# The residual summed into PSUM behind the first expert product, and normalised rows stored with even and odd columns apart

## The chip, the core and the metric

The kernel runs on one core of one Trainium2 chip. The core has a matrix engine (PE, TensorE), which loads a stationary operand (LDWEIGHTS) and streams a moving one through it (MATMUL) into PSUM; a vector engine (DVE), a scalar engine (ACT) and GpSimd (POOL), which read and write SBUF; and DMA queues, here fed almost wholly by SyncE (SP). The metric is the time of the whole program on the device in microseconds: 1033.31, the median of three runs of the kernel before (1030.22 to 1036.1).

## What is computed

Two decoder layers over 256 rows of 1024 columns, all in float32. Each layer is a set of four attention mixers, then a mixture of 32 experts of which each row uses two. The change lies in the experts. Cut to what matters:

```python
def hier_moe(h, w_coarse, b_coarse, w_fine, b_fine, w13, w2):
    lc = xf @ w_coarse + b_coarse
    grp = argmax(lc)                       # one of 4 groups
    lf = (xf @ w_fine + b_fine)[its group] # 8 experts in it
    top_p, top_e = top_k(softmax(lf), 2)
    wts = p_grp * top_p / sum(top_p)
    # per expert e: rows that chose it
    a, b = split(x_rows @ w13[e]);  y = (silu(a) * b) @ w2[e]
    # summed back into the rows with wts
x <- x + gate2(c) * hier_moe(rms_norm(x) * (1 + scale2(c)) + shift2(c))
```

## The kernel before, in words

The weights of the 32 experts of a layer are some 100 MB (32 experts of 2 MB in `w13` and 1 MB in `w2`), and all are read in each layer. They come in pieces of 1 MB into one of 8 ring buffers, or of 0.5 MB into one of 29 SBUF "pages" (128 by 1024 float32). SP issues these loads strictly in the order of a list (`advance`, line 302); a load waits until its buffer is free, which is when the last product that read the buffer's former piece is through (`done`, line 327). At most eight such loads are in flight.

All instructions are issued in the order in which the Python code calls them; each engine runs its own in that order, and semaphores order them between engines. The stretch that the change touches is `experts` (line 2071):

1. `router_part(l, 3)` transposes the last columns of the residual `X` on PE, ACT scales them into SBUF, and its second half `mm()` multiplies them with the router's weights.
2. `seeds(t)` opens the four PSUM banks `acc` in which the experts' results are summed: it multiplies the residual `X[t]` with the identity, two matmuls of 512 columns in float32 for each `t`, and so puts `x` itself into the sum. `seeds(0)` stands between the transposes and `mm()`, `seeds(1)` behind `route`.
3. `rstd_of` (DVE) gives `rs`, one factor a row. ACT writes `hh`, the rounded product `X * rs`, in four instructions of 512 columns; DVE writes `hl`, what the rounding left over, in eight of 256 columns (`lo(q)`: both `t` of one quarter `q`).
4. `route` (line 1852) is a chain of small DVE instructions from the router's sums to `rk`, the place of each row in its expert's list. `lo(0)` is called inside it, while PE adds up counts (`tri`). After it come `prep_sel(0)`, which builds 0/1 matrices `sel` from `rk`, and `lo(1)` to `lo(3)`, all on DVE.
5. `gather_bank` (line 1968) gathers the rows of the experts by matmul: for each block `kt` of 128 columns the stationary operand is a block of `hh` or `hl`, the moving one is `sel`. The block's columns are every second column of a range of 256 (`by_twos`, line 544), since the weights' rows are stored in pairs. Each bank of two blocks takes eight matmuls of 256 columns in the order hh, hl of `t=0`, hh, hl of `t=1`; four banks make a gather.
6. Eight steps `p` follow, each for four experts: `first(p, 0)`, `first(p, 1)` (products with `w13`), the gate on ACT and DVE, `second` (products with `w2`), and `scatter`, which adds into `acc`. Step 0 has `prep_t(0)` behind its first product (transposes of `sel`, slot weights). Gathers for later experts lie between the products.

Before the experts the mixers run an order of steps written out by hand; the change does not touch it.

Of the kernel before, what the change touches and what calls it, by code (L numbers as in the profile page):

```python
# [14 lines left out]
AF = mybir.ActivationFunctionType  # L15
OP = mybir.AluOpType
# [242 lines left out]
def kernel(ctx, tc, x_in, c_in, w_ada, b_ada, norm_gain, w_in, qk_gain, cmp_pe, cmp_w1, cmp_w2,  # L259
# [4 lines left out]
    V, A, G, T = (Engine(M, e, g) for e, g in zip("VAGP", (nc.vector, nc.scalar, nc.gpsimd, nc.tensor)))  # L264
# [7 lines left out]
    def dap(t, off, ap):  # L272
        return bass.AP(tensor=t.tensor, offset=t.offset + off, ap=ap)
# [3 lines left out]
    def T_(tag, shape, dt=FT):  # L277
        t = sb.tile(shape, dt, name=tag, tag=tag, bufs=TAGS[tag])
        M.tile(tag, TAGS[tag], t.tensor.name)
        return t  # L280

    def pg(shape, dt=FT):
        return T_("pg", shape, dt)

    def at(shape, dt=FT):
        t = ps.tile(shape, dt, name="at", tag="at", bufs=4)
        M.tile("at", 4, t.tensor.name)
        return t

    def mmb():  # L290
        t = ps.tile([128, 512], FT, name="mm", tag="mm", bufs=4)
        M.tile("mm", 4, t.tensor.name)
        return t
# [88 lines left out]
    X = {}  # L382
# [161 lines left out]
    def by_twos(v, kt):  # L544
        return v[:, 256 * (kt // 2) + kt % 2:256 * (kt // 2) + 256:2]
# [116 lines left out]
    def rstd_of(ss, eng=None):  # L662
        s2 = sm(2)
        V.tensor_reduce(s2, ss.rearrange("p (s t) -> p t s", t=2), axis=AX.X, op=OP.add)
        return rsqrt(s2, 2, 1.0 / D, eng or V)
# [39 lines left out]
    H = {}  # L705
# [757 lines left out]
    def expert(p, b, s):  # L1463

        return p + 16 * b + 8 * s
# [502 lines left out]
    def gather_bank(l, sel, n, q, xg, eng):  # L1968
        m = 64 * n
        p = at([128, 2, m])  # L1970
        for i in range(2):
            kt = 2 * q + i
            c = 0
            for t in range(2):
                for src in (H["hh"], H["hl"]):
                    T.matmul(p[:, i], by_twos(src[t], kt), sel[:, t].rearrange("p e s -> p (e s)"),
                             start=c == 0, stop=c == 3)
                    c += 1
        for i in range(2):
            kt = 2 * q + i  # L1980
            a, b = MOD[l, "A2"][:, kt:kt + 1], MOD[l, "sh2"][:, kt:kt + 1]
            if eng is V:
                V.tensor_scalar(xg[kt // 4][:, kt % 4], p[:, i], a, b, op0=OP.mult, op1=OP.add)
            else:
                A.activation(xg[kt // 4][:, kt % 4], p[:, i], AF.Identity, bias=b, scale=a)

    def first_half(p, m):
        t = T_("gt", [128, 512])
        A.activation(t, p, AF.Copy, scale=m)
        return t  # L1990
# [80 lines left out]
    def experts(l):  # L2071
        units = ada_pe(l, 5)

        def filler(n):
            for _ in range(n):
                units.pop(0)[1]()


        acc = {}

        def seeds(t):
            acc[t] = [mmb(), mmb()]
            for n in range(2):
                T.matmul(acc[t][n], ID, X[t][:, 512 * n:512 * n + 512], start=True, stop=False)

        filler(1)
        mm = router_part(l, 3)
        seeds(0)
        rs = rstd_of(H["ss"])
        for i in ("hh", "hl"):  # L2090
            H[i] = [pg([128, D], FR) for _ in range(2)]

        def lo(q):
            for t in range(2):
                c = slice(256 * q, 256 * q + 256)
                V.scalar_tensor_tensor(H["hl"][t][:, c], X[t][:, c], rs[:, t:t + 1], H["hh"][t][:, c], op0=OP.mult,
                                       op1=OP.subtract)

        for h in range(2):
            for t in range(2):  # L2100
                c = slice(512 * h, 512 * h + 512)
                A.activation(H["hh"][t][:, c], X[t][:, c], AF.Copy, scale=rs[:, t:t + 1])
        mm()
        filler(4)
        most, further, weights = route(l, rs, lo)
        seeds(1)

        NP = NE // 4
        SEL, ST, SW, SM, XG = {}, {}, {}, {}, {}

        def prep_sel(q):
            SEL[q], ST[q] = selection(rk[:, :, 4 * q:4 * q + 4], 4)
            XG[q] = [pg([128, 4, 256]) for _ in range(2)]

        def prep_t(q):
            selection_t(SEL[q], ST[q], 4)
            SW[q], SM[q] = slot_weights(SEL[q], W[:, :, :, 4 * q:4 * q + 4], 4)

        def prep_g(q, b, eng=None):
            gather_bank(l, SEL[q], 4, b, XG[q], eng or (V if b % 2 else A))  # L2120

        def first(p, b):
            q, i = divmod(p, 2)
            h = at([128, 512])
            for k in range(KT):
                for e in range(2):
                    key = "w13", l, expert(p, b, e), k // 4
                    c = 128 * i + 64 * e
                    T.matmul(h[64 * e:64 * e + 64], XG[q][k // 4][:, k % 4, c:c + 64], piece(key, (k % 4) * 512, 512),
                             start=k == 0, stop=k == KT - 1)  # L2130
                if k % 4 == 3:
                    for e in range(2):
                        done(("w13", l, expert(p, b, e), k // 4))
            return h

        def masks(p):
            return [SM[p // 2][:, b, p % 2:p % 2 + 1] for b in range(2)]

        def second(p, gT):
            ys = [at([128, 512]) for _ in range(2)]  # L2140
            for b in range(2):
                for n in range(2):
                    for k in range(2):
                        for e in range(2):
                            w = tiles[("w2", l, expert(p, b, e), k)]
                            T.matmul(ys[n][64 * e:64 * e + 64], gT[:, b, k, 64 * e:64 * e + 64],
                                     w[:, 512 * n:512 * n + 512], start=b == 0 and k == 0, stop=b == 1 and k == 1)
                    if b:
                        ys[n] = weighted(ys[n], SW[p // 2][:, p % 2:p % 2 + 1], MOD[l, "g2"][:, 512 * n:512 * n + 512])
                for k in range(2):  # L2150
                    for e in range(2):
                        done(("w2", l, expert(p, b, e), k))
            return ys

        prep_sel(0)
        most()
        for i in range(1, 4):
            lo(i)
        free["pg"] += P4[l]
        advance()  # L2160
        for b in range(4):
            prep_g(0, b, V if b > 1 else A)
        further()
        weights()
        ys = None
        for p in range(NP):
            q, i = divmod(p, 2)
            nxt = q + 1 < NP // 2
            if nxt and i == 0:
                prep_sel(q + 1)  # L2170
            if l + 1 < DEPTH and p == 2:
                load_weights(l + 1)
                load_cw2(l + 1)
            if l + 1 < DEPTH and p == NP - 1:
                tables()
            h = first(p, 0)
            if p == 0:
                prep_t(0)
            h = first_half(h, masks(p)[0])
            g = swiglu(first(p, 1), h, masks(p))  # L2180
            if p == 0:
                filler(2)
            if p:
                scatter(acc, ST[(p - 1) // 2][:, (p - 1) % 2], ys, False)
            if nxt:
                prep_g(q + 1, 3 * i)
            gT = hidden_t(g)
            if nxt and i == 0:
                prep_g(q + 1, 1)
                prep_g(q + 1, 2)  # L2190
            elif nxt:
                prep_t(q + 1)
            ys = second(p, gT)
        more_rounds(l, acc)
        scatter(acc, ST[q][:, i], ys, True)
        last = l == DEPTH - 1
        for t in range(2):
            X[t] = pg([128, D])
        for n in range(2):
            for t in range(2):  # L2200
                c = slice(512 * n, 512 * n + 512)
                if t:
                    A.activation(X[t][:, c], acc[t][n], AF.Copy)
                else:
                    V.tensor_copy(X[t][:, c], acc[t][n])
            for t in range(2):
                c = slice(512 * n, 512 * n + 512)
                if last:
                    nc.sync.dma_start(dap(out, t * 128 * D + 512 * n, [[D, 128], [1, 512]]), X[t][:, c])
            if not last:  # L2210
                turn(n)
# [56 lines left out]
```

## Time and profile before

| What | us |
|---|---|
| median of three runs | 1033.31 |
| the profiled execution's own time | 1038.59 |
| its span, first to last instruction | 1037.0 |
| PE busy | 982.9 |
| DVE busy | 538.9 |
| ACT busy | 406.5 |
| stretch of the experts in layer 0 / layer 1, from the first gather to the end of the results, about | 305 to 528 / 808 to 1037 |

The profile is of one execution. Almost all instructions carry the line of one helper (L253), so instructions are told apart by operation, shape and tile: `mm<-pg,K` are the seeds (identity `K`, residual in a page), `at<-pg` of 128x256 the gather, `at<-ring,pg` and `at<-pg` of 128x512 the products with `w13`, `at<-pg,gt` those with `w2`. A float32 matmul stands as two records. Matmuls overlap, so a record's length is longer than the step from one to the next; steps are read from a run of equal ones, as (length of the run minus length of one) divided by (count minus one). Times are from the start of the span.

### The profile page before, as it was taken

Reading aid. Unit: us, or ns where it says so; the run is one execution under the profiler, and the core shown is the slowest. Engines: PE = TensorE matmul, PEld = TensorE weight load, DVE = VectorE, ACT = ScalarE, POOL = GpSimd, SP = SyncE. Lnnn points to the kernel's source line nnn. Section 1 sums busy time; section 2 is a strip of 40 time slices with the busy share of each in tenths; the row PEclk is TensorE's granted clock in tenths of the full one; section 3 lists DMA queues with packets and bytes.
Section 4 is the critical chain, followed back from the end, with each engine's and each line's share of the span. In section 5 each row is a group of like instructions: output and inputs, shape, how many; then the busy total and the mean of one; then the engine's idle time right before and its main releaser. Section 6 shows DMA issues by size and latency. Waiting matters only on the chain.

```text
span 1037.0 us, 14343 instructions
## 1 busy us (share of the span) xinstructions
PE 982.9 (95%) x5175; PEld 601.1 (58%) x5176; DVE 538.9 (52%) x1237; ACT 406.5 (39%) x997; POOL 134.7 (13%) x271
## 2 busy tenths in 40 slices
PE   5999999999999999998899989999999999999996
PEld 2667777777774444442346857777878444444332
DVE  1667678979772222221156865987785523222112
ACT  1564857674442111110146557677354221111111
POOL 0031346302000000000001341603200000000000
PEclk7999999999999999999999989999999999999999
DMA  9977767478889999999997774566796999999995
GB/s 341 412 238 298 277 205 239 165 250 310 344 326 410 401 356 420 419 418 420 420 408 268 266 299 156 167 222 209 260 395 225 357 390 418 420 420 420 420 420 209
DMA packets 118462, 337.47 MB, mean 325 GB/s; under 512 B 13372, under 2 KB 31084, under 8 KB 118380
## 3 DMA queue, kind: packets, MB, share of 16 engines
q1 hardware_dynamic: 115670, 334.95, 84.3%
q10 hardware_dynamic: 2518, 1.47, 0.5%
q8 instruction: 44, 0.72, 0.3%
q14 instruction: 38, 0.31, 0.1%
q0 software_dynamic: 192, 0.02, 0.0%
HBM read 335.36 MB, written 1.05 MB: 324 GB/s over the span
## 4 chain that ended last, share of the span: by engine, by line
PE 57%; DMA 25%; DVE 8%; ACT 4%; POOL 3%; issue 2%; SPq 0%; ACTq 0%; DVEq 0%; POOLq 0%
PE mm L253 31%; PE at L253 26%; DMA pg<-in_w_dram 12%; DMA ring<-in_w_dram 11%; DVE pg L253 6%; ACT pg L253 3%; POOL sm L253 2%; DMA ring<-in_w_ada_dram 2%; DVE gt L253 1%; POOL pg L253 1%; ACT gt L253 1%; DMA rbs<-in_b_fine_dram 1%; DVE sm L253 1%; DVE smb L253 0%; POOL smb L253 0%
## 5 line engine op out<-in xcount | busy, mean ns | idle before, releaser
L253 PE MATMUL mm<-pg 128*128 128x512 f32 (+4 forms) x1856 | 434.1, 386 | 8.5 <-DVE pg L253 6.3
L253 PEld LDWEIGHTS mm<-pg 128*128 128x128 f32 x1856 | 329.3, 189 | 103.5 <-issue 22.8
L253 PE MATMUL at<-ring,pg 128*64 128x512 f32 (+3 forms) x888 | 239.3, 576 | 14.7 <-DMA ring<-in_w_dram 10.6
L253 DVE TENSOR_TENSOR pg<-ring,pg 128x512 fp32r<-128x512 f32 (+4 forms) x276 | 182.2, 696 | 63.6 <-ACT pg L253 62.8
L253 PE MATMUL at<-pg 128*64 128x512 f32 (+6 forms) x960 | 193.5, 390 | 2.2 <-DVE pg L253 1.1
L253 PEld LDWEIGHTS at<-ring,pg 128*64 128x64 f32 (+2 forms) x888 | 80.7, 139 | 134.0 <-issue 95.1
L253 ACT ACTIVATE pg<-ring 128x512 fp32r<-128x512 f32 (+4 forms) x276 | 148.6, 600 | 10.4 <-PE mm L253 3.6
L253 PEld LDWEIGHTS at<-pg 128*64 128x64 f32 (+3 forms) x960 | 97.4, 161 | 57.2 <-issue 41.2
L253 PE MATMUL at<-pg,gt 128*64 128x512 f32 x512 | 113.4, 595 | 2.7 <-ACT gt L253 2.7
L253 DVE SCALAR_TENSOR_TENSOR gt<-at,sm,gt 128x512 f32<-128x512 f32 x16 | 12.0, 751 | 191.4 <-PE at L253 191.4
L253 ACT ACTIVATE pg<-pg,sm 128x128 f32<-128x128 f32 (+2 forms) x168 | 70.5, 460 | 16.4 <-DVE sm L253 11.8
L253 PEld LDWEIGHTS at<-pg,gt 128*64 128x64 f32 x512 | 35.3, 137 | 68.5 <-issue 62.0
L253 ACT ACTIVATE pg<-at 128x512 f32<-128x512 f32 (+5 forms) x98 | 45.4, 495 | 64.4 <-PE at L253 64.1
L253 DVE SCALAR_TENSOR_TENSOR gt<-at,sm,pg 128x512 f32<-128x512 f32 x32 | 23.9, 748 | 86.4 <-PE at L253 86.4
L253 ACT ACTIVATE pg<-gt 128x512 fp32r<-128x512 f32 x32 | 20.2, 632 | 114.0 <-DVE gt L253 112.5
L253 PE MATMUL at<-K,pg 128*128 128x128 f32 (+1 forms) x356 | 55.3, 285 | 4.2 <-DVE pg L253 1.8
L253 DVE SCALAR_TENSOR_TENSOR pg<-ring,cs,pg 128x1024 f32<-128x1024 f32 x44 | 58.1, 1321 | 0.1
L253 ACT ACTIVATE gt<-mm 128x512 f32<-128x512 f32 x44 | 25.8, 596 | 78.1 <-PE mm L253 76.8
L253 PEld LDWEIGHTS at<-K,pg 128*128 128x128 f32 (+1 forms) x356 | 43.4, 150 | 18.9 <-issue 5.8
L253 ACT ACTIVATE gt<-gt 128x256 f32<-128x256 f32 x16 | 6.7, 419 | 119.1 <-DVE gt L253 119.1
L253 ACT ACTIVATE gt<-at,sm 128x512 f32<-128x512 f32 x16 | 11.0, 689 | 87.4 <-PE at L253 71.9
L253 POOL TENSOR_TENSOR pg<-pg,gt 128x512 f32<-128x512 f32 x16 | 29.6, 1875 | 108.1 <-DVE gt L253 108.1
(166 smaller groups left out, 669.5 us busy)
## 6 DMA issues: line engine op xcount, KB each, us to landing
pg<-in_w_dram SPq DMA_DIRECT2D x202, 512.0 KB, 11.6
ring<-in_w_dram SPq DMA_DIRECT2D x91, 1024.0 KB, 12.7
ring<-in_w_ada_dram SPq DMA_DIRECT2D x45, 1024.0 KB, 8.1
ring<-in_w_in_dram SPq DMA_DIRECT2D x33, 1024.0 KB, 5.0
ring<-in_cmp_w_dram SPq DMA_DIRECT2D x8, 1024.0 KB, 6.8
ring<-in_w_branch_dram SPq DMA_DIRECT2D x8, 1024.0 KB, 4.8
ring<-in_w_out_dram SPq DMA_DIRECT2D x8, 1024.0 KB, 4.9
ring<-in_w_in_dram SPq DMA_DIRECT2D x8, 976.0 KB, 7.6
```

What stands on the lines that cost most here:

```text
L253: return f(*args, **kw)
```

## The change

The two calls of `seeds` leave their places and stand together in step 0, behind `first(0, 0)` and `prep_t(0)`, ahead of the rest of the step. `hh` and `hl` are stored so that the 128 even columns of a range of 256 lie together, and then the odd ones: the gather's stationary block becomes contiguous, and ACT and DVE, which write the rows in the order of `X`, store neighbouring elements 128 elements apart. `lo` also reads `hh` in this way.

```diff
@@ gather_bank
-                    T.matmul(p[:, i], by_twos(src[t], kt), sel[:, t].rearrange("p e s -> p (e s)"),
+                    T.matmul(p[:, i], src[t][:, 128 * kt:128 * kt + 128], sel[:, t].rearrange("p e s -> p (e s)"),
@@ experts
         mm = router_part(l, 3)
-        seeds(0)
         rs = rstd_of(H["ss"])
...
+        def even_odd(v, q, n, inner):
+
+            s = "p (m c j) -> p m c j" if inner else "p (m j c) -> p m c j"
+            return v[:, 256 * q:256 * (q + n)].rearrange(s, j=2, c=128)
...
         def lo(q):
             for t in range(2):
-                c = slice(256 * q, 256 * q + 256)
-                V.scalar_tensor_tensor(H["hl"][t][:, c], X[t][:, c], rs[:, t:t + 1], H["hh"][t][:, c], op0=OP.mult,
-                                       op1=OP.subtract)
+                V.scalar_tensor_tensor(even_odd(H["hl"][t], q, 1, False), even_odd(X[t], q, 1, True), rs[:, t:t + 1],
+                                       even_odd(H["hh"][t], q, 1, False), op0=OP.mult, op1=OP.subtract)
 
         for h in range(2):
             for t in range(2):
-                c = slice(512 * h, 512 * h + 512)
-                A.activation(H["hh"][t][:, c], X[t][:, c], AF.Copy, scale=rs[:, t:t + 1])
+                A.activation(even_odd(H["hh"][t], 2 * h, 2, False), even_odd(X[t], 2 * h, 2, True), AF.Copy,
+                             scale=rs[:, t:t + 1])
         mm()
         filler(4)
         most, further, weights = route(l, rs, lo)
-        seeds(1)
...
             h = first(p, 0)
             if p == 0:
                 prep_t(0)
+                for t in range(2):
+                    seeds(t)
             h = first_half(h, masks(p)[0])
```

## Rows read from the trace of the kernel before

**Rows 1.** The page: what the DMA engines moved, in 40 equal slices of the span.

```profile
GB/s 341 412 238 298 277 205 239 165 250 310 344 326 410 401 356 420 419 418 420 420 408 268 266 299 156 167 222 209 260 395 225 357 390 418 420 420 420 420 420 209
```

**Rows 2.** The chain of waits in the experts of both layers: start, us, what.

```profile
305.48 44.80 PE at L253 x232
...
402.11 16.45 DMA ring<-in_w_dram
...
878.60 14.89 DMA ring<-in_w_dram
```

**Rows 3.** Stretches: length, busy us (instructions) of PE, PEld, DVE, ACT, POOL, clock, DMA share, GB/s.

```profile
340.00:344.00 4.00, 4.00 (x20) 1.29 (x18) 0.00 (x0) 0.46 (x1) 0.00 (x0) 1.00 0.87 316
...
840.00:844.00 4.00, 4.00 (x20) 1.29 (x18) 1.91 (x3) 0.63 (x1) 0.00 (x0) 1.00 0.92 310
...
402.00:510.00 108.00, 101.57 (x473) 42.21 (x471) 23.81 (x50) 14.10 (x25) 0.00 (x0) 1.00 1.03 420
```

**Rows 4.** Timeline of routing: start, us, instruction, count, [idle before it <- what ended it].

```profile
297.56 1.88 PE L253 MATMUL mm<-pg,K 128*128 128x512 f32 x4
...
300.08 0.48 DVE L253 SCALAR_TENSOR_TENSOR smb<-at,sm,rbias 128x40 f32<-128x40 f32 x2 [0.76 <-PE at L253]
...
303.31 0.87 DVE L253 SCALAR_TENSOR_TENSOR pg<-pg,sm 128x256 fp32r<-128x256 f32 x2
...
303.52 1.96 PE L253 MATMUL mm<-pg,K 128*128 128x512 f32 x4
...
305.34 2.44 DVE L253 SCALAR_TENSOR_TENSOR pg<-pg,sm 128x256 fp32r<-128x256 f32 x6
...
309.26 0.64 PE L253 MATMUL at<-ring,pg 128*64 128x512 f32 x1
...
803.52 0.48 DVE L253 SCALAR_TENSOR_TENSOR smb<-at,sm,rbias 128x40 f32<-128x40 f32 x2 [0.77 <-PE at L253]
```

**Rows 5.** Timeline of PE: two gather banks, and 24 products of contiguous blocks.

```profile
327.35 2.17 PE L253 MATMUL at<-pg 128*128 128x256 f32 x16
...
795.56 3.12 PE L253 MATMUL mm<-pg 128*128 128x256 f32 x24
```

**Rows 6.** Groups by shape, whole span: engine, operation, tiles, shape, count | busy us, mean ns | idle before.

```profile
L253 PE MATMUL mm<-pg,K 128*128 128x512 f32 x16 | 7.7, 603 | 0.0
...
L253 DVE TENSOR_REDUCE sm<-pg 128x8 f32<-128x256 f32 x6 | 2.5, 416 | 0.1
...
L253 DVE TENSOR_REDUCE sm<-pg 128x10 f32<-128x640 f32 x2 | 1.6, 810 | 0.0
L253 DVE TENSOR_REDUCE smb<-gt 128x40 f32<-128x320 f32 x2 | 1.6, 789 | 0.1
...
L253 DVE TENSOR_TENSOR pg<-pg,prm 128x240 f32<-128x240 f32 x4 | 2.1, 569 | 0.0
...
L253 DVE TENSOR_TENSOR pg<-pg,gt 128x256 f32<-128x256 f32 x8 | 3.4, 425 | 0.3
...
L253 DVE SCALAR_TENSOR_TENSOR pg<-pg,sm 128x256 fp32r<-128x256 f32 x16 | 6.6, 469 | 0.0
...
L253 ACT ACTIVATE pg<-pg,sm 128x512 fp32r<-128x512 f32 x8 | 5.1, 712 | 1.5 <-DVE sm L253 1.5
```

**Rows 7.** Timeline of SP: loads as issued, merged while their kind is the same.

```profile
333.14 3.38 SPq L320 DMA_DIRECT2D pg<-in_w_dram  x4
340.00 7.24 SPq L320 DMA_DIRECT2D ring<-in_w_dram  x5
```

**Rows 8.** Waits of SP from 318 to 348: us in total, times, longest.

```profile
SPq L320 <- PE at L253: 15.7, 6, 5.4
```

**Rows 9.** Timeline of PE: its longest idle time once under way.

```profile
606.37 6.44 PE L253 MATMUL at<-ring,pg 128*32 128x256 f32 x64 [3.58 <-POOL pg L253]
```

**Rows 10.** Stretches around that idle time, columns as in rows 3.

```profile
604.00:608.00 4.00, 1.63 (x16) 0.80 (x20) 4.00 (x6) 1.43 (x7) 3.69 (x7) 0.65 0.96 349
608.00:612.00 4.00, 4.00 (x44) 1.86 (x40) 0.88 (x3) 0.00 (x0) 2.39 (x11) 0.50 0.53 195
```

## The prediction

> **What bounds the kernel now.** I began with the page's line of what the DMA engines moved [rows 1]: two stretches of slices stand at about 420 GB/s, and they are the experts of the two layers. The stretch from 402 to 510 shows this at its plainest, 420 GB/s with a DMA share of 1.03 [rows 3]; nothing that engines do there can shorten it. So I asked the chain of waits where that phase begins [rows 2]. From 305.48 to 350, and on from there to 402.11, the chain lies on PE, and only from 402.11 (layer 0) and 878.60 (layer 1) on the transfers. In the first third of a layer's experts, then, the transfers follow PE: a buffer comes free when PE has read it. The windows say where this costs something [rows 3]. At 340 to 344 the DMA moved 316 GB/s and at 840 to 844 310, and (420 - 316) / 420 x 4 us = 1.0 us of transfer is lost there in either layer. The loads that end it are issued at 333.14 and 340.00 [rows 7], and SP waited for PE 15.7 us in six waits between 318 and 348 [rows 8]. So whatever makes PE later between the routing and 340 (840) makes the transfers later, and from there to the layer's end the DMA is full and gives nothing back. Then I read the timeline of the routing itself [rows 4].
>
> **The seeds leave the routing.** `seeds(0)` runs from 297.56 for 1.88 us [rows 4], between the transposes and the router's last products. DVE, which waits for these products, is idle 0.76 us before its first routing instruction at 300.08, ended by PE; in layer 1 it is 0.77. That idle time goes. What is late next is DVE itself: `rstd_of` keeps it busy until that idle time begins, so no more than 0.76 comes. `seeds(1)` runs from 303.52 to 305.48 and the gather's first product follows. The two matrices `sel` that the gather reads are written by DVE just before 305.34, when DVE goes on with `lo(1)` [rows 4]; the first two products need one of them, the third the other. Taking the seed away lets the first start some 0.2 us sooner, but the third by 0.12 at most, which I take. Gain if nothing else changed: 0.76 + 0.12 = 0.9 us a layer.
>
> **The seeds arrive in step 0.** They are 8 records in a layer (16 in the trace [rows 6]), with their own weight loads and no DMA. The step from one to the next is (1.88 - 0.60) / 3 = 0.43 us [rows 4, 6], so 8 x 0.43 = 3.4 us. Here PE has no idle time: the chain stays on PE without a break from 305.48 for 44.80 us [rows 2]. All 3.4 us are exposed. Queued behind them on PE are `first(0, 1)`, `hidden_t`, `second(0)` and `first(1, ...)`, whose ends free the buffers that SP waits for at 333.14 and 340.00. Only the releases by `first(0, 0)` come before the seeds and keep the gain. `X` also stays live longer, by two pages; these are not the next buffers that SP needs, and up to eight loads in flight cover the wait. If that cover fails SP stops for at most the 3.4 us that PE is later anyway, so I add nothing.
>
> **The contiguous stationary block.** Two gather banks take 2.17 us for 16 products, which is (2.17 - 0.29) / 15 = 0.125 us each, 0.29 being the record's length; contiguous blocks of the same shape take (3.12 - 0.29) / 23 = 0.123 [rows 5]. A block of every second column is thus no slower than 2 ns a product, and 128 products a layer give at most 0.3 us. I take 0.
>
> **The strided stores and reads.** Let d be what one `lo` instruction takes longer than its 469 ns [rows 6]. No row shows this instruction with neighbours 128 elements apart. Reductions give the nearest price: contiguous, (810 - 416) / 384 = 1.03 ns an element; with elements 40 apart, 789 ns for 320 of them, where 416 + 64 x 1.03 = 482 would be due, so 0.96 ns an element more. The 128x240 sum, which reads 16 elements apart, takes 569 against some 408 (425 less 16 x 1.03), so 0.67 more [rows 6]. For 256 elements that is 0.17 to 0.25 us. The lower end is d = 0, if two alternating runs cost nothing; below nothing is excluded, since contiguous is already the fastest form shown. The upper end is d = 0.4 to 0.5, if the store pays as the read does. I take d = 0.2, the value for the read alone.
>
> What the trace shows there is a price of about one further element time for each element that is far from the last. [...]
>
> On the path: `lo(0)`, two instructions in 0.87 us at 303.31, stands in DVE's queue ahead of the instruction that makes `rk` [rows 4], so 2d are paid at once. `lo(1)` to `lo(3)`, six in 2.44 us from 305.34, end at 307.78, while the gather's last bank is read until just before 309.26 [rows 4]; they have some 0.6 us of cover and then set the gather's end, because its last bank reads `hl` of the last quarter in its fourth of eight products. With d = 0.2: `lo(3)` ends at 307.78 - 0.76 + 8 x 0.2 = 308.62; four more products at 0.12 and the step to the first expert's product (0.3) put that at 309.4, against 309.26. So routing and gather together gain nothing: +0.1. With d = 0 the gather is bound by PE and its start, and they gain 0.9. With d = 0.4 they lose 1.7. ACT's four `hh` at 712 ns [rows 6] end at about 302; even doubled they would end near 304.5, the first half before `lo(0)` and the second before `lo(2)`, and nothing else on ACT is due before the gather's banks. I cost them at nothing; uncovered, it would be up to 2.5 us.
>
> **The sum.** PE reaches `second(0)` later by 3.4 + 0.1 = 3.5 us in each layer. Of that I take off 0.3 (0 to 1.0: the loss of 1.0 us in rows 3 may partly be the slow start of new loads behind old ones still running, which is the only slack there). 3.2 us a layer, 6.4 us in two. The profiled execution took 1038.59 (span 1037.0) and would take 1045.0. It lies 5.3 us above the median of the runs, 1033.31, and I carry the difference over to that: **1039.7 us**.
>
> **Rivals.**
> - The lines cost nothing (d = 0): 3.4 - 0.9 - 0.3 = 2.2 us a layer, 1037.7. For it: only reads, none of them alternating between two runs, show the price in rows 6. Against it: every distance shown there costs something.
> - The store pays like the read (d = 0.4): 3.4 + 1.7 - 0.3 = 4.8 a layer, 1043.0. No row shows a strided store, for or against. [...]
> - Not slower: loads in flight absorb the seeds. If at 333.14 and 340.00 (and in layer 1) the queue still holds 3.5 us of transfers beyond a new load's start, the later releases are not seen, and only the earlier ones by `first(0, 0)` count: 0.9 us a layer off, 1031.5. It decides from the point where the transfers in flight outlast the release by the seeds' 3.4 us. For it: between 318 and 333 the DMA runs on while SP waits. Against it: the loss at 340 to 344, which says the queue was dry without any delay.
> [...]
>
> **How the numbers follow.** Forecast 0.43, no price for lines 0.21, store pays too 0.17, absorbed 0.13, clock 0.06. A measurement of this kernel tells about 0.5% (5.2 us) from no change: below 1028.1 is faster, above 1038.5 slower. With some 2.5 us of scatter of a median, slower takes two thirds of the forecast, nearly all of the dear lines and the clock, and a third of the free lines: 0.56. Within 0.5%: 0.37. Faster: 0.07, the tail of the absorbed case and what I have not seen. The range runs from the absorbed case, 1031.5, to the clock's, 1046.
>
> **What would show it.** Seeds of 3.4 us behind the first product in PE's timeline, the first routing instruction of DVE 0.76 us earlier against the transposes, `lo` near 0.67 us instead of 0.47, gather steps still 0.12, and a larger loss of GB/s at 336 to 346 and 836 to 846. The prediction is wrong if these windows are not poorer than before, or if `second(0)` starts less than 2 us later behind the router's transposes.

## The result, and the profile after

The changed kernel takes 1039.34 us (median of 8 runs, 1038.13 to 1043.67), the kernel before on the same chip 1033.26 (8 runs, 1030.22 to 1036.22): ratio 1.0065, 95% interval 1.0047 to 1.0083, or 6.1 us more. The forecast was 1039.7. The ratios below leave out one run, of e2, that took 1346.85 us at a mean granted clock of 0.683.

The two profiled executions can't be set against each other as wholes: 1038.13 after, 1038.59 before. In that of before TensorE's clock stood at half for a time near the start (granted clock 0.57 from 14 to 30 us) and between the layers [rows 10]; in that of after it did neither. So I measure inside a layer, from the router's transposes (start 296.99 and 800.43 before, 294.30 and 795.55 after), and all the times "behind the transposes" below are that.

The page, what the DMA engines moved after; it answers to [rows 1]:

```profile
GB/s 355 411 260 290 278 213 208 165 287 311 344 323 369 383 375 420 419 418 420 420 409 271 264 331 160 197 177 240 281 362 236 369 329 418 420 420 420 420 420 211
```

Slices 13 and 14 read 369 and 383, where they were 410 and 401, slice 33 reads 329, where it was 390; slice 15 goes the other way, 375 for 356, and is taken up at the end. The full phases at 420 are as before. The stretches say it closer (columns as in [rows 3]):

```profile
301.00:305.00 4.00, 3.09 (x14) 3.12 (x15) 3.93 (x12) 1.63 (x5) 2.15 (x4) 0.57 1.02 414
...
333.00:337.00 4.00, 4.00 (x20) 1.29 (x18) 0.49 (x1) 0.00 (x0) 0.00 (x0) 1.00 0.64 228
337.00:341.00 4.00, 4.00 (x22) 1.37 (x20) 2.31 (x4) 1.26 (x2) 0.00 (x0) 1.00 0.97 371
341.00:345.00 4.00, 4.00 (x22) 1.36 (x20) 0.00 (x0) 0.00 (x0) 0.00 (x0) 1.00 0.73 239
402.00:510.00 108.00, 102.60 (x480) 42.63 (x476) 24.34 (x50) 14.06 (x25) 0.00 (x0) 1.00 1.03 420
...
802.00:806.00 4.00, 2.80 (x13) 2.83 (x14) 3.93 (x12) 1.77 (x6) 2.10 (x4) 0.67 1.02 413
...
834.00:838.00 4.00, 4.00 (x20) 1.29 (x18) 0.05 (x1) 0.00 (x0) 0.00 (x0) 1.00 0.40 125
838.00:842.00 4.00, 4.00 (x22) 1.36 (x20) 2.61 (x4) 1.26 (x2) 0.00 (x0) 1.00 0.85 292
```

Where [rows 3] lose transfers (316 and 310 GB/s), the changed kernel falls to 228 and 239, and in layer 1 to 125; the stretch from 402 to 510 is at 420 in both, so what is lost is not won back there. The first line holds what I had given 0.06: the granted clock is 0.57 in the four us in which the gather begins, and 0.67 in those of layer 1.

The chain of waits after (start, us, what), which answers to [rows 2]:

```profile
301.91 13.39 PE at L253 x72
315.30 3.54 PE mm L253 x8
318.83 1.43 PE at L253 x5
...
803.20 13.54 PE at L253 x72
816.74 3.54 PE mm L253 x8
820.27 1.86 PE at L253 x7
```

The seeds stand in the chain by themselves, 3.54 us in either layer, in the middle of what was one unbroken stretch of PE. The timeline of layer 0 after, which answers to [rows 4]:

```profile
296.74 0.43 DVE L253 SCALAR_TENSOR_TENSOR smb<-at,sm,rbias 128x40 f32<-128x40 f32 x2
...
299.91 1.15 DVE L253 SCALAR_TENSOR_TENSOR pg<-pg,sm 128x256 fp32r<-128x256 f32 x2
...
301.91 6.01 PE L253 MATMUL at<-pg 128*128 128x256 f32 x33 [1.64 <-DVE pg L253]
...
302.10 3.16 DVE L253 SCALAR_TENSOR_TENSOR pg<-pg,sm 128x256 fp32r<-128x256 f32 x6
...
307.29 0.64 PE L253 MATMUL at<-ring,pg 128*64 128x512 f32 x1
```

DVE's first routing instruction has no idle time ahead of it any more; `lo(0)` takes 1.15 us for 0.87, the other six 3.16 for 2.44. PE is idle 1.64 us ahead of the gather, where `seeds(1)` ran, and the gather's 33 records take 6.01 us; before the same run of 33 took 4.83:

```profile
305.06 4.83 PE L253 MATMUL at<-pg 128*128 128x256 f32 x33
```

The groups by shape after, which answer to [rows 6]:

```profile
L253 DVE SCALAR_TENSOR_TENSOR pg<-pg,sm 128x256 fp32r<-128x256 f32 x16 | 8.6, 654 | 0.0
L253 ACT ACTIVATE pg<-pg,sm 128x512 fp32r<-128x512 f32 x8 | 8.3, 1186 | 1.5 <-DVE sm L253 1.5
```

And the waits of SP over the same 30 us of layer 0, which answer to [rows 8]: 20.7 us for 15.7, the longest 7.5 for 5.4.

```profile
SPq L320 <- PE at L253: 20.7, 6, 7.5
```

### The profile page after: what moved, and what is told of

Same layout as the page of the kernel before. It is cut to its first block, busy times and chain, and to the rows that moved or that the text cites. A ratio compares the mean times of both kernels' runs of the same rounds, so it can differ in the third digit from the quotient of the medians.

```text
span 1036.4 us, 14346 instructions
## 1 busy us (share of the span) xinstructions
PE 983.8 (95%) x5175; PEld 602.3 (58%) x5176; DVE 540.6 (52%) x1237; ACT 408.4 (39%) x997; POOL 134.6 (13%) x271
## 4 chain that ended last, share of the span: by engine, by line
PE 67%; DMA 15%; DVE 10%; ACT 4%; POOL 2%; issue 2%; SPq 0%; ACTq 0%; DVEq 0%; POOLq 0%
PE at L253 35%; PE mm L253 32%; DVE pg L253 7%; DMA ring<-in_w_dram 7%; DMA pg<-in_w_dram 6%; ACT pg L253 3%; DVE gt L253 1%; POOL sm L253 1%; DMA ring<-in_w_ada_dram 1%; POOL pg L253 1%; ACT gt L253 1%; DVE sm L253 1%; DMA rbs<-in_b_fine_dram 1%; DVE smb L253 0%; POOL smb L253 0%
## 5 line engine op out<-in xcount | busy, mean ns | idle before, releaser
L253 PE MATMUL mm<-pg 128*128 128x512 f32 (+4 forms) x1856 | 433.4, 386 | 8.4 <-DVE pg L253 5.9
L253 PEld LDWEIGHTS mm<-pg 128*128 128x128 f32 x1856 | 328.8, 189 | 103.1 <-issue 22.8
L253 PE MATMUL at<-ring,pg 128*64 128x512 f32 (+3 forms) x888 | 236.1, 561 | 11.4 <-DMA ring<-in_w_dram 9.4
L253 DVE TENSOR_TENSOR pg<-ring,pg 128x512 fp32r<-128x512 f32 (+4 forms) x276 | 183.1, 699 | 59.2 <-ACT pg L253 58.4
L253 PE MATMUL at<-pg 128*64 128x512 f32 (+6 forms) x960 | 195.7, 394 | 5.5 <-DVE pg L253 4.4
L253 PEld LDWEIGHTS at<-ring,pg 128*64 128x64 f32 (+2 forms) x888 | 79.7, 135 | 128.4 <-issue 92.8
L253 ACT ACTIVATE pg<-ring 128x512 fp32r<-128x512 f32 (+4 forms) x276 | 148.4, 599 | 10.7 <-DVE pg L253 4.8
L253 PEld LDWEIGHTS at<-pg 128*64 128x64 f32 (+3 forms) x960 | 99.8, 164 | 61.1 <-issue 43.8
L253 PE MATMUL at<-pg,gt 128*64 128x512 f32 x512 | 113.4, 595 | 2.7 <-ACT gt L253 2.7
L253 DVE SCALAR_TENSOR_TENSOR gt<-at,sm,gt 128x512 f32<-128x512 f32 x16 | 12.0, 751 | 196.8 <-PE at L253 196.8
L253 ACT ACTIVATE pg<-pg,sm 128x128 f32<-128x128 f32 (+2 forms) x168 | 73.3, 480 | 16.3 <-DVE sm L253 11.6
L253 PEld LDWEIGHTS at<-pg,gt 128*64 128x64 f32 x512 | 35.3, 137 | 68.6 <-issue 62.0
L253 DVE SCALAR_TENSOR_TENSOR gt<-at,sm,pg 128x512 f32<-128x512 f32 x32 | 24.0, 749 | 86.4 <-PE at L253 86.4
L253 ACT ACTIVATE pg<-at 128x512 f32<-128x512 f32 (+5 forms) x98 | 45.2, 493 | 60.0 <-PE at L253 59.8
L253 ACT ACTIVATE pg<-gt 128x512 fp32r<-128x512 f32 x32 | 20.1, 630 | 114.0 <-DVE gt L253 114.0
L253 PE MATMUL at<-K,pg 128*128 128x128 f32 (+1 forms) x356 | 55.3, 286 | 4.2 <-DVE pg L253 1.8
L253 DVE SCALAR_TENSOR_TENSOR pg<-ring,cs,pg 128x1024 f32<-128x1024 f32 x44 | 57.1, 1297 | 0.1
L253 ACT ACTIVATE gt<-gt 128x256 f32<-128x256 f32 x16 | 6.7, 417 | 124.5 <-DVE gt L253 124.5
L253 ACT ACTIVATE gt<-mm 128x512 f32<-128x512 f32 x44 | 25.8, 596 | 73.7 <-PE mm L253 72.5
L253 PEld LDWEIGHTS at<-K,pg 128*128 128x128 f32 (+1 forms) x356 | 43.4, 150 | 18.9 <-issue 6.1
L253 ACT ACTIVATE gt<-at,sm 128x512 f32<-128x512 f32 x16 | 11.0, 687 | 87.4 <-PE at L253 71.9
L253 POOL TENSOR_TENSOR pg<-pg,gt 128x512 f32<-128x512 f32 x16 | 30.1, 1903 | 107.6 <-DVE gt L253 107.6
```

Source lines behind the costliest of these rows:

```text
L253: return f(*args, **kw)
```

## The experiments

One table holds what the traces say. "Second" is where `second(0)` starts, "end" where the last 24 products of the layer start (the line `5.42 PE at L253 x24` in the chain, at 518.39 and 1020.75 before; in layer 0 of e10, where the chain does not pass there, their start in the timeline, 514.11), both in us behind the transposes, layer 0 / layer 1. "Against before" is the sum of the two ends less that of before, 441.72. The clock is the lowest granted during the gather. Each row's traces are of one execution; the ratios are of 4 to 12 runs. Ratios are to runs of the kernel before on the same chip, with their 95% interval.

| kernel | clock | second | end | against before | ratio |
|---|---|---|---|---|---|
| before | 1.0 | 32.47 / 32.47 | 221.40 / 220.32 | | |
| changed | 0.5 | 36.70 / 36.89 | 223.96 / 224.65 | +6.9 | 1.0065 [1.0047, 1.0083] |
| e1 seeds moved alone | 0.5 | 36.79 / 36.74 | 224.49 / 224.51 | +7.3 | 1.0063 [1.0041, 1.0086] |
| e2 layout alone | 1.0 | 32.76 / 32.72 | 221.01 / 220.50 | -0.2 | 1.0011 [0.9996, 1.0026] |
| e3 seeds in step 5 | 1.0 | 31.74 / 31.70 | 221.74 / 220.87 | +0.9 | 1.0028 [1.0007, 1.0048] |
| e4 changed, gap filled | 1.0 | 35.55 / 35.55 | 223.65 / 223.37 | +5.3 | 1.0049 [1.0031, 1.0067] |
| e5 changed, seeds twice | 0.5 | 40.27 / 40.43 | 228.13 / 228.30 | +14.7 | 1.0141 [1.0117, 1.0165] |
| e6 seeds(0) in step 1 | 1.0 | 31.76 / 31.75 | 220.55 / 220.36 | -0.8 | 0.9983 [0.9970, 0.9996] |
| e7 changed, reads apart | 1.0 | 35.25 / 35.21 | 222.76 / 223.43 | +4.5 | 1.0058 [1.0035, 1.0080] |
| e8 both seeds in step 1 | 0.5 | 33.21 / 33.18 | 223.60 / 222.90 | +4.8 | 1.0026 [1.0010, 1.0042] |
| e9 seeds(0) in step 0 | 1.0 | 33.57 / 33.57 | 220.95 / 221.54 | +0.8 | 1.0002 [0.9984, 1.0020] |
| e10 seeds(0) in step 3 | 1.0 | 31.76 / 31.76 | 220.27 / 220.43 | -1.0 | 0.9983 [0.9966, 0.9999] |

The first four ask which half of the change costs, and whether the clock does.

**e1, the seeds moved, the old layout.**

```diff
-        seeds(0)
...
-        seeds(1)
...
                 prep_t(0)
+                for t in range(2):
+                    seeds(t)
```

> Only the seeds move (both behind the first product of step 0); rows are stored as before. Theory A (3.4 us of seeds stand open on PE ahead of the releases that the transfers wait for): second(0) starts 3.5 to 4 us later behind the router's transposes than before (32.5 us there), the time is 5 to 7 us above before, nearly all of the change's 6.1. Rival B (the stores 128 elements apart are the cost): no more than 1 us above before, or 1 to 2 us below it, since the routing loses 0.9 us a layer. Theory C on the clock (PE idle ahead of the gather lets the granted clock fall): gather steps of 0.21 instead of 0.12 us at its start, as in the changed kernel; without it all at 0.12.

Ratio 1.0063: as much as the whole change, without the layout. It holds what the move does to the routing and to the clock as well.

**e2, the layout, the seeds where they were.** (`by_twos` out, `even_odd` in, both calls of `seeds` at their old lines.)

```diff
-                    T.matmul(p[:, i], by_twos(src[t], kt), ...
+                    T.matmul(p[:, i], src[t][:, 128 * kt:128 * kt + 128], ...
...
+                A.activation(even_odd(H["hh"][t], 2 * h, 2, False), even_odd(X[t], 2 * h, 2, True), ...
```

> Only the layout changes (even and odd columns apart); the seeds stand where they stood before. Theory A: lo about 0.65 and hh about 1.19 us as in the changed kernel, the first expert's product some 0.3 us later behind the transposes (12.3 before), time 0 to 1 us above before. Rival B: 4 to 6 us above before. Theory C: with seeds(1) ahead of the gather PE is not idle, the clock stays at 1.00 and all gather steps are 0.12 us.

Ratio 1.0011, and the interval holds 1. In its groups by shape the stores do cost, as in the changed kernel:

```profile
L253 DVE SCALAR_TENSOR_TENSOR pg<-pg,sm 128x256 fp32r<-128x256 f32 x16 | 8.6, 658 | 0.0
L253 ACT ACTIVATE pg<-pg,sm 128x512 fp32r<-128x512 f32 x8 | 8.3, 1189 | 1.5 <-DVE sm L253 1.5
```

but `second(0)` is only 0.27 us later, and the ends are -0.4 and +0.2 off. The rival that puts the loss on the strided stores (4 to 6 us) has fallen: the interval ends at 2.7 us.

**e3, the seeds late.** The old layout; the first scatter opens the banks, and the seeds are added in step 5.

```diff
-        seeds(0)
...
-        seeds(1)
...
+            if p == 1:
+                for t in range(2):
+                    acc[t] = [mmb(), mmb()]
             if p:
-                scatter(acc, ST[(p - 1) // 2][:, (p - 1) % 2], ys, False)
+                scatter(acc, ST[(p - 1) // 2][:, (p - 1) % 2], ys, False, p == 1)
+            if p == 5:
+                for t in range(2):
+                    seeds(t)
```

> Rows stored as before; the seeds are taken from routing and from step 0 and added in step 5, where PE waits for weights; the first scatter opens the banks instead. Theory A: second(0) starts 0 to 1 us earlier than before (32.5 behind the transposes), since routing is 0.9 us shorter and the clock may take back up to 1.3; time between 2 us below and 1 us above before. If the seeds cost their 3.4 us wherever they stand on PE: 5 to 7 us above before, as the change. Theory C: gather steps of 0.21 us at its start.

Ratio 1.0028, 2.9 us: most of the loss is gone with the place, not all, and the time is above the 1 us that was the upper end expected. `second(0)` is 0.7 to 0.8 us earlier, as expected. The profiled execution has +0.9 us, the interval 0.7 to 4.9 us, so its lower end only agrees. PE's idle time ahead of the gather is there as in e1, and yet the clock held in this execution, as the timeline of PE shows:

```profile
301.24 4.75 PE L253 MATMUL at<-pg 128*128 128x256 f32 x33 [1.47 <-DVE pg L253]
```

**e4, the changed kernel with PE kept at work.** Two products with the identity, into a bank that nothing reads, where `seeds(1)` stood.

```diff
         most, further, weights = route(l, rs, lo)
+        spare = mmb()
+        for n in range(2):
+            T.matmul(spare, ID, X[1][:, 512 * n:512 * n + 512], start=True, stop=True)
```

> The changed kernel with two more identity matmuls (1.7 us, into a spare bank that nothing reads) where seeds(1) stood ahead of the gather. Theory C (the clock fell because PE was idle there, and that cost 1.3 us a layer): granted clock 1.00 through the gather, all its steps 0.12 us, the first expert's product about 1.2 us sooner behind the transposes than the 13.0 of the changed kernel, time 2 to 3 us below the changed kernel's. Without C (the fall has another cause): clock and steps as in the changed kernel, the time the same or up to 1 us above it.

The stretch in which the gather begins, for the changed kernel's clock of 0.57:

```profile
304.00:308.00 4.00, 4.00 (x30) 3.47 (x28) 4.00 (x10) 1.88 (x6) 2.15 (x4) 1.00 1.02 414
```

The clock holds, and the first product starts 11.83 us behind the transposes in both layers, against 12.98 and 13.17 in the changed kernel: 1.15 and 1.34 us back, the 1.3 expected. Of that 0.3 and 1.3 reach the ends. The ratios (1.0049 for 1.0065) go the same way, but by 1.7 us, less than the 2 to 3 expected, and their intervals overlap; it is the trace that carries this, not the timed runs. Since the clock also held in e3 without a filler, one execution of e4 does not show by itself that the filler is why. The mean granted clock of each run says a little more. None of the 20 runs of the changed kernel, e1 and e5 has a mean above 0.997, and eight of the twelve of e4 have; but so have only two of the twelve of e2, where PE is not idle there. Falls elsewhere in the span count in such a mean too.

The others ask how much of PE's time is exposed, where, and what the stores pay for.

**e5, the dose doubled.**

```diff
-        def seeds(t):
-            acc[t] = [mmb(), mmb()]
+        def seeds(t, banks=None, stop=False):
+            acc[t] = banks or [mmb(), mmb()]
...
                 for t in range(2):
-                    seeds(t)
+                    seeds(t, None, True)
+                for t in range(2):
+                    seeds(t, acc[t])
```

> The changed kernel, with the eight records of the seeds written a second time at the same place in each layer (the second set overwrites the first). Theory A (each seed record behind the first product is exposed for its whole step of 0.43 us): 8 x 0.43 = 3.4 us a layer more than the changed kernel, 6.9 in all, about 1.0125 to 1.0135 times the kernel before; second(0) starts about 3.5 us later behind the router's transposes than the 36.7 us of the changed kernel. Rival (the seeds' place costs, a wait or a late release, and not their length; or transfers absorb a part): no more than half of that, below 1.0100.

The chain of waits:

```profile
315.41 6.97 PE mm L253 x16
...
822.47 6.97 PE mm L253 x16
```

6.97 for 3.54 us; `second(0)` 3.6 and 3.5 us later than in the changed kernel, the ends 4.2 and 3.7. Ratio 1.0141, 0.0076 or 7.9 us above the changed kernel's, where 6.9 were due (some 5 to 11 by the two intervals): nothing shows that any of it is absorbed. The stretch of 8 us from 36 us behind the transposes of layer 1, in the kernel before, the changed kernel and e5 (columns as in [rows 3]), shows the dose in the transfers:

```profile
836.43:844.43 8.00, 8.00 (x40) 2.68 (x38) 2.80 (x4) 1.26 (x2) 0.00 (x0) 1.00 0.97 322
```

```profile
831.55:839.55 8.00, 8.00 (x43) 3.25 (x43) 1.90 (x4) 1.87 (x4) 0.00 (x0) 1.00 0.51 178
```

```profile
837.17:845.17 8.00, 8.00 (x49) 4.92 (x49) 2.46 (x6) 4.04 (x8) 0.00 (x0) 1.00 0.27 85
```

322, 178 and 85 GB/s: against 420 that is (420 - x) / 420 x 8 = 1.9, 4.6 and 6.4 us of transfer lost. Over the first 90 us behind the transposes the DMA moved 386 GB/s in layer 0 and 393 in layer 1 before, 372 and 371 in the changed kernel, and 355 in both in e5. Against 420 that is 7.3 and 5.8, 10.3 and 10.5, and 13.9 us lost; the differences, 3.0 and 4.7, then 3.6 and 3.4 us, are close to those of the ends (2.6 and 4.3, then 4.2 and 3.7).

**e6, seeds(0) in step 1; seeds(1) stays ahead of the gather.** The old layout.

```diff
-        seeds(0)
...
             if p:
+            if p == 1:
+                seeds(0)
                 scatter(acc, ST[(p - 1) // 2][:, (p - 1) % 2], ys, False)
```

> The kernel before (old layout), where only seeds(0) is moved, into step 1 just ahead of the first scatter; seeds(1) stays in the routing and so keeps PE at work ahead of the gather. Theory A (the routing's gain is real, the clock holds while PE has work ahead of the gather, and 1.7 us of seeds 25 us later stand where the transfers are full): first product 0.7 us earlier behind the transposes, clock 1.00 through the gather, no loss of transfers beyond that of before: 0 to 0.7 us a layer faster, ratio 0.9985 to 1.0000. Rival (PE's work costs wherever it stands in the first steps): 1.7 - 0.7 = 1.0 us a layer slower, ratio about 1.002.

Ratio 0.9983, interval 0.9970 to 0.9996: 1.8 us less than the kernel before, and less than the changed kernel. `second(0)` is 0.7 us earlier, as expected, the clock holds, and the stretch 36 us behind the transposes of layer 1 is not poorer than before:

```profile
823.70:831.70 8.00, 8.00 (x50) 4.87 (x50) 2.22 (x5) 3.50 (x7) 0.00 (x0) 1.00 0.86 336
831.70:839.70 8.00, 8.00 (x40) 2.73 (x38) 2.80 (x4) 1.26 (x2) 0.00 (x0) 1.00 0.92 338
```

The 8 us ahead of it are poorer, 336 where the kernel before has 420 (828.43 to 836.43). e10, whose seed comes later still, has 345 there, so it is not the seed that does it; but transfers are lost beyond those of before, against what was expected, and the ends (0.85 us earlier in layer 0, 0.04 later in layer 1) show the gain in one layer alone.

**e7, the changed kernel with strided reads for strided stores.** The same bytes at the same places: ACT and DVE store without gaps and read `X` at every second element.

```diff
-            s = "p (m c j) -> p m c j" if inner else "p (m j c) -> p m c j"
+            s = "p (m c j) -> p m j c" if inner else "p (m j c) -> p m j c"
```

> The changed kernel, but ACT and DVE write the rows contiguous and read X at every second element instead (8 bytes apart), so the same bytes come to lie at the same places. [...] If any access that is not contiguous pays: lo near 650, hh near 1190, as in the changed kernel. Time in both cases within 0.2% of the changed kernel (1.0050 to 1.0065 of the kernel before), since the layout alone moved it by 0.1%.

```profile
L253 DVE SCALAR_TENSOR_TENSOR pg<-pg,sm 128x256 fp32r<-128x256 f32 x16 | 6.6, 469 | 0.0
L253 ACT ACTIVATE pg<-pg,sm 128x512 fp32r<-128x512 f32 x8 | 5.6, 782 | 1.5 <-DVE sm L253 1.5
```

`lo` is back at 469 ns, `hh` at 782 (712 before, 1186 changed). The time, 1.0058, stays near that of the change. The two cases were 469 and 712 ns, the times of before, if reads 8 bytes apart cost nothing, and 650 and 1190, those of the change, if they cost what neighbours 512 bytes apart do. `lo` falls on the first: it takes 469 ns with reads 8 bytes apart, and 654 with neighbours 512 bytes apart, 1.4 times as long. `hh` is near it: its reads 8 bytes apart cost 70 ns on 712, its stores 512 bytes apart 474. In `lo` both the store and the read of `hh` were 512 bytes apart, and no run separates them; in `hh` it was the store alone.

**e8, both seeds in step 1.** The old layout, PE idle ahead of the gather as in the change.

```diff
-        seeds(0)
...
-        seeds(1)
...
             if p:
+            if p == 1:
+                for t in range(2):
+                    seeds(t)
                 scatter(acc, ST[(p - 1) // 2][:, (p - 1) % 2], ys, False)
```

> The kernel before (old layout) with both seeds in step 1, just ahead of the first scatter, 25 us later than the change puts them and behind the releases by second(0). Theory A (only PE work ahead of those releases costs; the clock falls at the gather since PE is idle there, 1.3 us, and the routing gains 0.8): about +0.5 us a layer, ratio 1.000 to 1.002, and the stretch 33 to 45 us behind the router's transposes is no poorer in transfers than in the kernel before. Rival (3.4 us of PE cost the same anywhere in the first two steps): as the seeds alone in step 0, ratio 1.0050 to 1.0065.

Ratio 1.0026 (1.0010 to 1.0042), between the two expectations; the interval still holds the upper end of the first. `second(0)` is 0.7 us later (clock down, routing up), the ends 2.2 and 2.6: so, if the 0.7 come through whole, some 1.5 to 1.9 of the 3.4 us of seeds behind it do so too in this execution. The stretch that was to be no poorer, 33 to 45 us behind the transposes, is poorer in layer 1: 283 GB/s for 353 before (317 in e10). The claim that only work ahead of the releases by `second(0)` costs was too sharp. The runs, at 2.7 us, are below the 4.8 of this trace, so the share that comes through is not settled.

**e9 and e10, half the dose, and later still.** The old layout; `seeds(1)` stays ahead of the gather, `seeds(0)` goes to the change's place (e9) or behind the third scatter (e10, where the first scatter opens its two banks).

```diff
-        seeds(0)
...
                 prep_t(0)
+                seeds(0)
```

> The kernel before (old layout), where seeds(0) alone goes to the place of the change, in step 0 behind the first product; seeds(1) stays in the routing. Half the dose, and PE has work ahead of the gather. Theory A (each microsecond of PE there is exposed, and the clock's fall needs the idle time): clock 1.00 through the gather, second(0) 0.7 earlier and 1.7 later, so at about 33.5 us behind the transposes; 0.7 to 1.0 us a layer slower, ratio 1.0012 to 1.0020. Rival (the first two microseconds are absorbed by transfers in flight, and only what lies beyond them costs): no slower than the kernel before, ratio 0.9983 to 1.0000.

`second(0)` is at 33.57, as expected. The ratio, 1.0002 with 0.9984 to 1.0020, can't tell the two apart. The ends are -0.4 and +1.2; against e10, which has no seed there, +0.7 and +1.1 for 1.7 us of PE. That would be about half of the 1.7 us absorbed, but it rests on one execution of each, and the two ratios, 0.0019 apart, have intervals that overlap: how much of so small a dose is exposed is not shown.

```diff
-        seeds(0)
...
+            if p == 1:
+                acc[0] = [mmb(), mmb()]
             if p:
-                scatter(acc, ST[(p - 1) // 2][:, (p - 1) % 2], ys, False)
+                scatter(acc, ST[(p - 1) // 2][:, (p - 1) % 2], ys, False, p == 1)
+            if p == 3:
+                seeds(0)
```

> The kernel before (old layout) with seeds(0) behind the third scatter, in step 3; the first scatter opens the two banks of these rows; seeds(1) stays in the routing. Theory A (the routing's 0.7 us a layer is kept whole once the seed stands where the transfers are full): as with seeds(0) in step 1 or up to 0.7 us a layer better, ratio 0.9970 to 0.9985. Rival (a seed that late costs too, by the pages of X held longer or by PE at the layer's end): 0.9995 to 1.0010.

Ratio 0.9983 again: step 3 is no better than step 1. That the gain is the 0.7 us that the routing gives in each layer fits its size, but is not shown: as in e6 the end is earlier in layer 0 (by 1.1 us) and not in layer 1 (0.1 later).

## Why the prediction was right, step by step

**What bounds the kernel: right, but for one stretch of layer 0.** In the first third of a layer's experts transfers follow PE, and from there on the DMA is full, except in layer 0 from 70 to 90 us behind the transposes (see the sum below). e5 shows it at its plainest: 3.4 us more of PE in step 0, 3.7 to 4.2 us later at the layer's end.

**Seeds in step 0, 3.4 us exposed: right.** From the first product to `second(0)` it is 20.21 us before (32.47 - 12.26) and 23.72 after, in both layers: 3.51 more. e1 shows that moving the seeds, with what that does to the routing and the clock, is the whole of the change's cost.

**Seeds out of the routing, 0.76 and 0.12 gained: right in place, a little high.** DVE's first routing instruction starts 2.44 us behind the transposes (296.74 - 294.30), 3.09 before: 0.65 earlier. The gather starts 7.62 us behind the transposes, 8.08 before: 0.46 less with the longer `lo(0)` in it. In e6, with the old `lo`, it starts at 7.44 and the first product comes 0.71 earlier. In e1, where `seeds(1)` is gone too, the gather starts no sooner (7.44 and 7.39), so the 0.12 did not come.

**The strided stores: the length right, the way to the path wrong.** I forecast 0.67 us for `lo`, it is 0.654. But from one to the next it is (3.16 - 0.654) / 5 = 0.50 us, against (2.44 - 0.469) / 5 = 0.39 before: 0.11 more, not the 0.2 that I charged for each of eight. `lo` therefore doesn't end the gather as I had it: where the clock holds (e4) the first product comes 0.43 us earlier than before, where I had 0.1 later. My reason for the size, that reads pay and stores don't, is not borne out: in `hh` only the store is strided, and it went from 712 to 1186 ns.

**The contiguous block gains nothing: right.** Two gather banks of e2 take 2.15 us for 2.17 [rows 5].

**The clock: the step that failed.** The gather's steps were to stay at 0.12 us. I had the clock's fall as a rival at 0.06, because the idle time I expected, 2 us, is less than the 3.58 of [rows 9]. The clock went to 0.5 for 3.4 us in both layers of the changed kernel, where PE was idle 1.64 and 1.67 us ahead of the gather. I had also priced it too high: 4 x 0.35 + 4 x 0.50 = 3.4 us a layer by the clocks of [rows 10], and twice that on the forecast is the upper end of the range, 1046. No run shows such a price; e4 gives 1.15 and 1.34.

**The sum was right partly by offset.** Routing and gather together: +0.1 forecast; -0.43 by e4 and +1.15 to +1.34 for the clock, so +0.72 and +0.91. `second(0)`: +3.5 forecast, +4.23 and +4.42 measured. At the end: 3.2 a layer forecast, 2.56 and 4.33 measured, 6.9 in all for 6.4; the runs say 6.1. That layer 0 gives back 1.7 us and layer 1 only 0.1 I had not foreseen: I took off 0.3 each, an estimate of mine for a slow start of new loads, which no run shows. The traces show where most of it lies, from 70 to 90 us behind the transposes of layer 0, before and after:

```profile
366.99:386.99 20.00, 20.00 (x106) 9.62 (x104) 3.81 (x7) 3.87 (x8) 0.00 (x0) 1.00 0.92 336
```

```profile
364.30:384.30 20.00, 20.00 (x108) 9.57 (x106) 4.42 (x9) 4.26 (x8) 0.00 (x0) 1.00 0.96 362
```

Against 420 that is 4.0 and 2.8 us lost: the DMA was not full there, though I had it full from 340 on, and the changed kernel loses 1.2 us less. The delay of PE need not be why: in all the other kernels, e6 and e10 with an earlier PE among them, the same 20 us have 349 to 362 GB/s, and the 336 of before may be scatter of its one execution.

**The rivals.** No price for strided access (d = 0, the "free lines"): refuted by the 654 ns (0.11 us from step to step). Store pays: it does in `hh`, where it is hidden, but `lo` stays at 654 ns and not at 870. Absorbed by transfers in flight: refuted for the change by its 6.1 us, and by e5, where the second dose comes through; open for a dose of 1.7 us (e9).

**What stays open:** why the clock fell in the changed kernel, e1, e5 and e8 and not in e3 and e7, whose idle time ahead of the gather is the same 1.4 to 1.5 us as in e1; how often it falls in the timed runs; why e3's runs are slower than its trace and e8's faster; and how much of a dose of 1.7 us is exposed.

## What to carry to other kernels

Work that can stand anywhere belongs where its engine has no one waiting: ahead of the gather the seeds cost 0.7 us of waiting a layer, behind the first product 3.5 us; half of them, one to three steps later (e6, e10), nothing that was seen. A filler moved away can also let PE's clock fall, as it did, to 0.5, in four of six executions here, so look at the idle time that it leaves. And an instruction that grows on an engine off the path may cost next to nothing (e2: 0.3 us at `second(0)`, nothing clear in the time), however large its own change is.

## What was not expected of the hardware

- The granted clock of TensorE fell to 0.5 for 3.4 us after PE had run five products of 128x16 and then been idle 1.44 to 1.69 us. The fall came between 0.3 us before the gather's first product (layer 0 of the changed kernel) and 1.7 us behind it (layer 1 of e5), so in part when PE was at work again. In two of six executions with this idle time (e3 and e7) it did not fall.
- Neighbours 512 bytes apart: ACT 712 to 1186 ns for 512 float32 (stores), DVE 469 to 654 ns for 256 (store and one read; 0.11 us from step to step). Reads 8 bytes apart: 469 ns on DVE, 782 on ACT.
